# Output bias on GpSimd, later sample state, later stage transposes and a split last norm in an eight-core decoder layer

## The chip, the cores and the metric

The kernel runs on all eight cores of one Trainium2 chip. The prompt batch of eight sequences is split, one sequence of 2048 tokens per core, with 16 decode ("sample") tokens beside it. The metric is the device time of the slowest core in microseconds (us). Some executions fall into a slower state in which the cores of one die, or of both, run at a lower granted clock. A time given for a run is the median of its fast executions.

The engines in the profile: PE is TensorE's matmul, PEld its weight load, DVE is VectorE, ACT is ScalarE, POOL is GpSimd, SP is SyncE. L457 means line 457 of that kernel's file. The change shifts line numbers, so the same work has two names:

| work | before | changed |
|---|---|---|
| up/gate matmuls (SwiGLU) | L457 | L482 |
| silu of the gate (ACT) | L462 | L487 |
| down matmuls | L521 | L546 |
| combined input projection | L576 | L604 |
| width-31 conv as matmuls | L694 | L722 |
| output projection | L806 | L834 |
| bias matmuls / bias add | L809 | L846 |
| rstd (one over the standard deviation) of the conv norm (POOL) | L768, L770 | L796, L798 |
| transposes of normalised or loaded tiles | L396 | L395 |

## The reference, cut to what matters

```python
x = layer_norm(ALPHA * x + 0.5 * swiglu(x, f1_wg, f1_wu, f1_wd), ln_f1_g, ln_f1_b)
# token_mixers: z = x @ w_in + b_in, split into five parts
#   u = a_val * sigmoid(a_gate);  ua = silu(layer_norm(conv31(u) + b_dw_a))
#   v = g_c * b_val;              ub = g_b * conv3(v)
m = concatenate([ua, ub]) @ w_o + b_o
x = layer_norm(ALPHA * x + m, ln_mix_g, ln_mix_b)
x = layer_norm(ALPHA * x + 0.5 * swiglu(x, f2_wg, f2_wu, f2_wd), ln_f2_g, ln_f2_b)
# sample tokens: the same, the convolutions continue from state_conv_a and state_conv_b
```

d_model is 1024, the SwiGLU width 2816, one layer.

## The kernel before

A core's tokens are worked in two blocks. The stages follow one another on PE: start and first up stage, first down stage, first mixer stage, second down stage, second mixer stage, third down stage, last up and down stages, last norm. A mixer stage weaves the mixer of one block (conv part "C", output-projection part "E") into the up matmuls of another. The weave is made by `merge`: each side step carries a number, the share of up groups that may follow it. An up group is the 16 gate and up matmuls of one weight chunk on one group of tokens. In the program every engine has its own list of instructions, and a DMA stands in the list of the engine that issues it: most weights in POOL's, almost everything else in SP's.

```python
        def merge(items, side):
            credit = 0.0
            items = list(items)
            for th, gap in side:
                th()
                credit += gap
                while credit >= 1.0 - 1e-9 and items:
                    items.pop(0)()
                    credit -= 1.0
            # ... the rest of the items
```

The output bias was added by two rank-2 matmuls per tile (the bias split in two bf16 rows), behind the 16 matmuls of the output projection:

```python
            def S3(t):
                # ...
                    for k in (4, 5, 6, 7, 0, 1, 2, 3):
                        for h in range(2):
                            e.matmul(ps[...], lhsT=lhs(k), rhs=wo[:, k, ...], start=(k == 4), stop=False)
                    for h in range(2):
                        ins = e.matmul(ps[...], lhsT=ones2[0:2, :n], rhs=bo2[0:2, ...], start=False, stop=True)

            def A(i):
                if 0 <= i - 1 < nt:
                    S2(tl[i - 1])          # transposes back, silu on ACT
                if i < nt:
                    S1(tl[i])              # transposes, statistics on DVE, rstd on POOL, normalise on ACT
                    xslot[i] = load_xr(tl[i], ...)     # reload the residual
```

The conv input takes a detour: DVE writes u, SP stores it to memory (`uscr`), SP loads it back four times, shifted (`R2`), and only then the conv matmuls of that channel group (`tD`) can run, some steps later. Of the steps, `tA` stores u and `tB` reloads it; there are four channel groups, called channels below. The start of a mixer stage:

```python
        side = [(lambda: None, 2.0), (lambda p=pend: xpose(*p, mb()), 1.0)] + mixer(0, 0, 0.8, 0.9, 1.5)
        merge(up_items(0, 1), side)
        # ...
        side = [(lambda: None, 1.0), (lambda p=pend: xpose(*p, mb()), 0.5)] + mixer(1, 1, 0.5, 0.6, 1.0)
        merge(up_items(1, 0), side)
```

`xpose(*pend)` transposes the last normalised tile of the down stage before. At the start, `consts()` made the two bias rows with DVE operations and small SP DMAs; behind them, SP issued the loads of the sample state.

Of the kernel before, what the change touches and what calls it, by code (L numbers as in the profile page):

```python
# [6 lines left out]
F32 = mybir.dt.float32  # L7
# [5 lines left out]
D = 1024  # L13
# [158 lines left out]
def build_nc():  # L172
# [36 lines left out]
    with stack:  # L209
# [7 lines left out]
        E4 = sb("E4", [128, 4, 32], F32)  # L217
        dgb = sb("dgb", [128, 2, 8 * 128], BF16)
        bo2 = sb("bo2", [2, D], BF16)
        ones2 = sb("ones2", [2, 128], BF16)  # L220
        lnb = sb("lnb", [128, 2, D], F32)
# [200 lines left out]
        def ln_tail(ctx):  # L422
# [6 lines left out]
                op0=ALU.mult, op1=ALU.add), reads=[("xr", s), ("rs", m), ("lnb", 1)], writes=[("xr", s)])  # L429

        def store_xr(t, s, dst, wtok=()):
            n = tok(t)[1]
            P.op("sp", lambda e: e.dma_start(out=dst, in_=xr[:n, s, :]), reads=[("xr", s)], writes=list(wtok),
                 dma="xr_st%d" % s)
# [59 lines left out]
        def down(which, b, in_scale, eps, final, npar=0, aux=None):  # L494
# [40 lines left out]
            for i, t in enumerate(tl):  # L535
                n = tok(t)[1]
                if npar:
                    if i == 0:
                        for c in range(0, 16, 2):
                            for ii in range(npar):  # L540
                                mms(ii, c, c + 2)
                    mms(i, 16 if i < npar else 0, NFC)
                elif i == 0:
                    for c in range(0, NFC, 2):
                        mms(i, c, c + 2)
                else:  # L546
                    mms(i, 0, NFC)
                pre(i + nsk)
                if pend is not None:
                    xpose(*pend, tb())  # L550
                    pend = None
                for h in aux.get(i, ()):
                    h()
                ctx = ln_head(t, slots[i], pairs[i], in_scale, eps)
                ln_tail(ctx)
                if final:
                    (tok0, n) = tok(t)
                    store_xr(t, slots[i], yp[tok0:tok0 + n, :] if t < 16 else ys[:, :])
                else:
                    c = cast_xb(t, slots[i])  # L560
                    store_xr(t, slots[i], spill(0, t), [("x1", t)])
                    pend = (t, c)
            return pend

        def unit_C(u):
# [112 lines left out]
            def tD0(ch):  # L678
                ds_ = ch % 2
                wcol = C_WP + ch * 32  # L680
                P.op("dve", lambda e: e.tensor_tensor(
                    out=dgb[:, ds_, :].rearrange("p (q g c) -> p q g c", q=8, g=4),
                    in0=E4[:, :, :].unsqueeze(1).to_broadcast([128, 8, 4, 32]),
                    in1=cst[:, wcol:wcol + 32].rearrange("p (q g) -> p q g", q=8).unsqueeze(3).to_broadcast([128, 8, 4, 32]),
                    op=ALU.mult), reads=["E4", "cst"], writes=[("dgb", ds_)])

            def tD(ch):
                bk = mb()
                ds_ = ch % 2

# [22 lines left out]
            for ch in range(4):  # L713
                prev = ch - 1
                out.append(th(lambda ch=ch: tD0(ch), lambda ch=ch: tA(ch)))
                if prev >= 0:
                    out.append(th(lambda p=prev: tD(p)))
                out.append(th(lambda ch=ch: tB(ch), lambda ch=ch: rep_in(ch), lambda ch=ch: tB2(ch)))
                out.append(th(lambda ch=ch: tG(ch)))
# [17 lines left out]
        def unit_E(u):  # L737
# [57 lines left out]
            def S3(t):  # L795
# [7 lines left out]
                def pe(e):  # L803
                    for k in (4, 5, 6, 7, 0, 1, 2, 3):
                        for h in range(2):
                            e.matmul(ps[:n, (4 + h) * 512:(5 + h) * 512], lhsT=lhs(k), rhs=wo[:, k, h * 512:(h + 1) * 512],  # L806
                                     start=(k == 4), stop=False)
                    for h in range(2):
                        ins = e.matmul(ps[:n, (4 + h) * 512:(5 + h) * 512], lhsT=ones2[0:2, :n],  # L809
                                       rhs=bo2[0:2, h * 512:(h + 1) * 512], start=False, stop=True)  # L810
                    return ins
                rt = [("catS", k) for k in range(8)] if t == 16 else \
                    [("catA", k, t % 4) for k in range(4)] + [("catB", par, k) for k in range(4)]
                P.op("pe", pe, reads=rt + ["wo", "ones2", "bo2"] + ME, writes=pst(4, 2))

            def A(i):
                if 0 <= i - 1 < nt:
                    S2(tl[i - 1])
                if i < nt:
                    S1(tl[i])  # L820
# [126 lines left out]
        P.op("dve", lambda e: e.tensor_copy(out=ident_bf[:], in_=ident[:]), reads=["ident"], writes=["ident_bf"])  # L947
        P.op("dve", lambda e: e.memset(ones2[:], 1.0), writes=["ones2"])
        P.op("dve", lambda e: e.memset(haloU[:], 0.0), writes=[("haloU", c) for c in range(4)])
# [5 lines left out]
        def consts():  # L955
# [3 lines left out]
                                                  op0=ALU.mult), reads=["cst"], writes=["hbg"])  # L959
            s1, s2 = xrr(), xrr()  # L960
            hl = xb[0:1, 0, :]
            c = xbr()
            c2_ = xbr()
            P.op("sp", lambda e: e.dma_start(out=xr[0:1, s1, :], in_=bod), writes=[("xr", s1)], dma="c_bo")
            P.op("dve", lambda e: e.tensor_copy(out=xb[0:1, c, :], in_=xr[0:1, s1, :]), reads=[("xr", s1)], writes=[("xb", c)])
            P.op("dve", lambda e: e.tensor_copy(out=xr[0:1, s2, :], in_=xb[0:1, c, :]), reads=[("xb", c)], writes=[("xr", s2)])
            P.op("dve", lambda e: e.tensor_tensor(out=xb[0:1, c2_, :], in0=xr[0:1, s1, :], in1=xr[0:1, s2, :], op=ALU.subtract),
                 reads=[("xr", s1), ("xr", s2)], writes=[("xb", c2_)])
            P.op("sp", lambda e: e.dma_start(out=bo2[0:1, :], in_=xb[0:1, c, :]), reads=[("xb", c)], writes=[("bo2", 0)],
                 dma="c_bo2a")  # L970
            P.op("sp", lambda e: e.dma_start(out=bo2[1:2, :], in_=xb[0:1, c2_, :]), reads=[("xb", c2_), ("bo2", 0)],
                 writes=["bo2"], dma="c_bo2b")

# [18 lines left out]
        ss = sample_state()  # L992
        side = [(lambda: (consts(), ss[0](), load_ln(0)), 2)]
        for i in range(11):
            side.append((lambda i=i: load_wd(0, i), 1.0))
            side.append((ss[1 + i] if i < len(ss) - 1 else (lambda: None), 2.2))
        merge(up_items(0, 0)[4:], side)
# [20 lines left out]
        while wstate["f"] < NWIN:  # L1018
            fetch_win()
        side = [(lambda: None, 2.0), (lambda p=pend: xpose(*p, mb()), 1.0)] + mixer(0, 0, 0.8, 0.9, 1.5)  # L1020
        merge(up_items(0, 1), side)
        load_ln(0)
        pend = down(0, 1, 2.0 * ALPHA, 4.0 * EPS, False, npar=3)
        side = [(lambda: None, 1.0), (lambda p=pend: xpose(*p, mb()), 0.5)] + mixer(1, 1, 0.5, 0.6, 1.0)
        merge(up_items(1, 0), side)
# [77 lines left out]
```

## Time and profile before

| | before |
|---|---|
| time | 1313.61 and 1314.78 us; a third run, 1399.56, was slow |
| spans of the cores in the profiled run | 1295.9 to 1312.2 us |
| PE busy | 95% |

Three lines of the page of the kernel before: the span, the busy times (us, share, instructions), and the shares of the chain of waits that ended last.

```profile
span 1312.2 us, 20168 instructions; the slowest of 8 cores (1295.9 to 1312.2 us)
PE 1240.5 (95%) x7262; PEld 645.5 (49%) x7262; DVE 527.4 (40%) x856; ACT 273.9 (21%) x460; POOL 211.3 (16%) x361
PE 87%; DMA 6%; DVE 2%; issue 2%; ACT 1%; POOL 1%; SPq 0%; POOLq 0%; DVEq 0%; ACTq 0%
```

PE is the bound. What can be won is PE work and PE waits. The view of waits, PE alone, kernel before (who waited for what: us in total, times, longest):

```profile
PE ps L893 <- DMA sb_hT<-sca: 12.9, 1, 12.9
PE ps L396 <- ACT sb_xb L384: 11.4, 5, 5.1
PE ps L396 <- DMA sb_hT<-xp: 9.3, 2, 8.3
PE ps L694 <- DMA sb_RW<-uscr: 6.7, 2, 5.1
PE ps L457 <- ACT sb_sg L462: 2.2, 3, 1.4
```

The first is the sample state, the fourth the conv input, the last the silu. The timeline around the start, kernel before (start in us, duration, engine, line, operation, output<-input, count; in brackets the idle time before it and what ended it):

```profile
39.98 0.64 SPq L969 DMA_DIRECT2D sb_bo<-sb_xb  x1
46.28 0.52 SPq L971 DMA_DIRECT2D sb_bo<-sb_xb  x1
46.85 3.33 SPq L880 DMA_DIRECT2D sb_hT<-sca  x4
61.90 1.03 PE L893 MATMUL ps<-sb_ident,sb_hT 128*128 128x128 f32 x4 [12.90 <-DMA sb_hT<-sca]
```

SP issued the sample load (46.85) only behind the two bias rows (39.98 and 46.28), which waited for DVE. PE timeline of one output projection, kernel before:

```profile
377.44 3.62 PE L806 MATMUL ps<-sb_wo,sb_RW 128*128 128x512 bf16 x16
380.99 0.60 PE L809 MATMUL ps<-sb_bo,sb_ones 2*128 2x512 bf16 x2
381.52 2.56 PE L457 MATMUL ps<-sb_xT,sb_ring 128*128 128x352 bf16 x16
```

Matmuls overlap in the record, so the cost of a group is read from start to start: the two bias matmuls take 381.52 - 380.99 = 0.53 us.

### The profile page before, as it was taken

To read this page: it belongs to the slowest core of one execution; us is meant where nothing else is said; L and a number is where in the kernel's file an instruction comes from. 1 tells how busy PE (TensorE), PEld (TensorE's weight loads), DVE (VectorE), ACT (ScalarE), POOL (GpSimd) and SP (SyncE) were. 2 spreads that over 40 slices of the span, in tenths; PEclk is the share of its full clock that TensorE was granted. 3 is DMA by queue.
4 is the path that set the end of the run, shared out by engine and by line. 5 is a ranking of instruction groups with operands and counts; after the bars stand their busy time and mean duration, and the time that the engine had idled before them with its cause. 6 is when DMAs were issued, how large, how long until landed. Compare 5 with 4: busy or idle time off the path is not lost.

```text
span 1312.2 us, 20168 instructions; the slowest of 8 cores (1295.9 to 1312.2 us)
## 1 busy us (share of the span) xinstructions
PE 1240.5 (95%) x7262; PEld 645.5 (49%) x7262; DVE 527.4 (40%) x856; ACT 273.9 (21%) x460; POOL 211.3 (16%) x361
## 2 busy tenths in 40 slices
PE   5599999999999999998989899999999999999996
PEld 4244444445555556553444344445444456666443
DVE  0222124544445544515544345543633632222454
ACT  2111112231123313301121123313420011111000
POOL 2011102211122112111111112102220110000011
PEclk9899999999999999999999999999999999999999
DMA  9686769448865686793237856546777344442122
GB/s 137 132 180 112 123 111 179 135 118 148 168 124 126 136 164 118 159 198 107 67 102 142 163 110 134 123 89 132 148 177 146 128 113 80 69 79 33 51 82 81
DMA packets 65172, 161.54 MB, mean 123 GB/s; under 512 B 6882, under 2 KB 17506, under 8 KB 65059
## 3 DMA queue, kind: packets, MB, share of 16 engines
q0 software_dynamic: 36832, 90.75, 42.8%
q1 hardware_dynamic: 28243, 69.51, 16.6%
q8 instruction: 60, 0.98, 0.3%
q14 instruction: 37, 0.30, 0.1%
HBM read 223.24 MB, written 28.70 MB: 192 GB/s over the span
## 4 chain that ended last, share of the span: by engine, by line
PE 87%; DMA 6%; DVE 2%; issue 2%; ACT 1%; POOL 1%; SPq 0%; POOLq 0%; DVEq 0%; ACTq 0%
PE ps L457 44%; PE ps L521 23%; PE ps L576 10%; PE ps L806 4%; PE ps L694 2%; DMA sb_RW<-wd 2%; PE ps L396 2%; DMA sb_RW<-uscr 1%; DMA sb_hT<-sca 1%; DMA uscr<-sb_RW 1%; DMA sb_ring<-wgu 1%; PE ps L809 1%; PE ps L783 1%; PE ps L758 1%; DVE sb_xr L427 1%
## 5 line engine op out<-in xcount | busy, mean ns | idle before, releaser
L457 PE MATMUL ps<-sb_xT,sb_ring 128*128 128x352 bf16 (+3 forms) x3568 | 639.3, 338 | 13.9 <-ACT sb_xT L400 7.0
L457 PEld LDWEIGHTS ps<-sb_xT,sb_ring 128*128 128x128 bf16 x3568 | 347.9, 99 | 284.8 <-issue 30.6
L521 PE MATMUL ps<-sb_RW,sb_hT 128*128 128x512 bf16 (+1 forms) x1496 | 327.4, 380 | 0.6 <-DMA sb_RW<-wd 0.6
L464 DVE TENSOR_TENSOR sb_hT<-sb_sg,ps 128x352 bf16<-128x352 f32 (+3 forms) x223 | 129.0, 579 | 456.9 <-PE ps L457 399.1
L521 PEld LDWEIGHTS ps<-sb_RW,sb_hT 128*128 128x128 bf16 (+1 forms) x1496 | 145.2, 98 | 175.7 <-issue 3.5
L462 ACT ACTIVATE sb_sg<-ps 128x352 f32<-128x352 f32 (+3 forms) x223 | 113.5, 510 | 497.0 <-PE ps L457 395.9
L576 PE MATMUL ps<-sb_xT,sb_wring 128*128 128x512 bf16 (+1 forms) x800 | 150.4, 340 | 2.0 <-DVE sb_hT L464 1.3
L408 DVE SCALAR_TENSOR_TENSOR sb_xr<-sb_xr,ps 128x1024 f32<-128x1024 f32 (+1 forms) x51 | 62.2, 1219 | 172.4 <-PE ps L521 154.1
L337 POOL DMA_DIRECT2D sb_ring<-wgu x90 | 49.9, 558 | 412.4 <-PE ps L457 373.9
L576 PEld LDWEIGHTS ps<-sb_xT,sb_wring 128*128 128x128 bf16 x800 | 68.5, 98 | 78.6 <-issue 5.5
L416 POOL TENSOR_SCALAR sb_mv<-sb_mv 128x1 f32<-128x1 f32 (+1 forms) x51 | 16.0, 314 | 383.5 <-DVE sb_mv L414 383.4
L427 DVE SCALAR_TENSOR_TENSOR sb_xr<-sb_xr,sb_mv,sb_lnb 128x1024 f32<-128x1024 f32 (+1 forms) x51 | 65.5, 1284 | 21.4 <-POOL sb_mv L418 18.4
L350 POOL DMA_DIRECT2D sb_wring<-win x80 | 43.4, 543 | 174.1 <-PE ps L576 152.0
L384 ACT ACTIVATE sb_xb<-sb_xr 128x1024 bf16<-128x1024 f32 (+1 forms) x34 | 36.0, 1058 | 164.2 <-DVE sb_xr L427 164.2
L412 DVE BATCH_NORM_STATS2 sb_stt<-sb_xr 128x6 f32<-128x512 f32 (+1 forms) x102 | 65.6, 684 | 5.3
L424 DVE SCALAR_TENSOR_TENSOR sb_xr<-sb_xr,sb_mv,sb_lnb 128x1024 f32<-128x1024 f32 (+1 forms) x51 | 66.0, 1294 | 4.1
L400 ACT ACTIVATE sb_xT<-ps 128x1024 bf16<-128x1024 bf16 (+1 forms) x51 | 48.7, 978 | 72.0 <-PE ps L396 71.8
L806 PE MATMUL ps<-sb_wo,sb_RW 128*128 128x512 bf16 x256 | 57.9, 379 | 0.0
L418 POOL TENSOR_TENSOR sb_mv<-sb_mv,sb_neghalf 128x1 f32<-128x1 f32 (+1 forms) x51 | 53.8, 1055 | 7.9 <-POOL sb_mv L416 0.9
L806 PEld LDWEIGHTS ps<-sb_wo,sb_RW 128*128 128x128 bf16 x256 | 24.9, 98 | 29.0 <-issue 0.4
L694 PE MATMUL ps<-sb_RW,sb_dgb 128*32 128x512 bf16 x512 | 31.8, 392 | 7.5 <-DMA sb_RW<-uscr 6.7
L396 PE MATMUL ps<-sb_ident_bf,sb_xb 128*128 128x128 bf16 (+1 forms) x272 | 20.7, 219 | 11.4 <-ACT sb_xb L384 11.4
(82 smaller groups left out, 394.5 us busy)
## 6 DMA issues: line engine op xcount, KB each, us to landing
sb_ring<-wgu POOLq DMA_DIRECT2D x86, 512.0 KB, 5.8
sb_wring<-win POOLq DMA_DIRECT2D x80, 256.0 KB, 5.5
sb_RW<-wd POOLq DMA_DIRECT2D x33, 512.0 KB, 8.2
sb_RW<-uscr SPq DMA_DIRECT2D x64, 135.0 KB, 4.5
sb_xr<-xp SPq DMA_DIRECT2D x16, 512.0 KB, 7.1
x1s<-sb_xr SPq DMA_DIRECT2D x16, 512.0 KB, 3.0
sb_xr<-x1s SPq DMA_DIRECT2D x16, 512.0 KB, 6.5
x2s<-sb_xr SPq DMA_DIRECT2D x16, 512.0 KB, 3.1
```

The costliest lines, as they stand in the source:

```text
L408: P.op("dve", lambda e: e.scalar_tensor_tensor(out=xr[:n, s, :], in0=xr[:n, s, :], scalar=in_scale, in1=ps[:n, bk * 512:(bk + 2) * 512], o ...
L412: P.op("dve", lambda e, h=h: e.bn_stats(out=stt[:n, m, h, :], in_=xr[:n, s, h * 512:(h + 1) * 512]), reads=[("xr", s)], writes=[("stt", m, ...
L418: P.op("pool", lambda e: e.tensor_tensor(out=mv[:n, m, 2:3], in0=mv[:n, m, 3:4], in1=neghalf[:n, 0:1], op=ALU.pow), reads=[("ve", m), "neg ...
L424: P.op("dve", lambda e: e.scalar_tensor_tensor(out=xr[:n, s, :], in0=xr[:n, s, :], scalar=mv[:n, m, 0:1], in1=lnb[:n, 0, :], op0=ALU.subtr ...
L427: P.op("dve", lambda e: e.scalar_tensor_tensor(out=xr[:n, s, :], in0=xr[:n, s, :], scalar=mv[:n, m, 2:3], in1=lnb[:n, 1, :], op0=ALU.mult, ...
L457: ins = e.matmul(bank(bk, n), lhsT=ring[:, s, c:c + 128], rhs=xT[:, k, tok0:tok0 + n], start=(k == 0), stop=(k == KC - 1))
L462: P.op("act", lambda e: e.activation(out=sg[:, q, :n], in_=bank(bg, n), func=AF.Silu), reads=pst(bg), writes=[("sg", q)])
L464: P.op("dve", lambda e: e.tensor_tensor(out=hT[:, f, l0:l0 + n], in0=sg[:, q, :n], in1=bank(bu, n), op=ALU.mult), reads=[("sg", q)] + pst( ...
L521: ins = e.matmul(ps[:n, (yb + h) * 512:(yb + h + 1) * 512], lhsT=hT[:, f, l0:l0 + n], rhs=wd[:, f, h * 512:(h + 1) * 512], start=(f == 0), ...
L576: ins = e.matmul(bank(bk, n), lhsT=wring[:, slot, k * 128:(k + 1) * 128], rhs=xT[:, k, tok0:tok0 + n], start=(k == 0), stop=(k == KC - 1))
L694: ins = e.matmul(ps[32 * g_:32 * g_ + 32, bk * 512:(bk + 1) * 512], lhsT=dgb[:, ds_, q * 128 + 32 * g_: q * 128 + 32 * g_ + 32], rhs=R2[:, ...
L806: e.matmul(ps[:n, (4 + h) * 512:(5 + h) * 512], lhsT=lhs(k), rhs=wo[:, k, h * 512:(h + 1) * 512], start=(k == 4), stop=False)
```

## The change

Its intent: take the bias off PE; let the sample loads be issued at once and use their data later; let PE do other work while the last tile of a stage is still being normalised; and start the last norm on the half that is finished first. To make room for the bias row in all partitions, the conv weights (`dgb`) lose their second buffer, and are built a step later.

```diff
-                            e.matmul(..., start=(k == 4), stop=False)
-                    for h in range(2):
-                        ins = e.matmul(..., lhsT=ones2[0:2, :n], rhs=bo2[0:2, ...], start=False, stop=True)
+                            ins = e.matmul(..., start=(k == 4), stop=(k == 3))
...
             def A(i):
                 if 0 <= i - 1 < nt:
                     S2(tl[i - 1])
+                if 0 <= i - 1 < nt:
+                    n, s = tok(tl[i - 1])[1], xslot[i - 1]
+                    P.op("pool", lambda e: e.tensor_tensor(out=xr[:n, s, :], in0=xr[:n, s, :], in1=boa[:n, :], op=ALU.add), ...)
                 if i < nt:
                     S1(tl[i])
                     xslot[i] = load_xr(tl[i], spill(0, tl[i]), [("x1", tl[i])])
...
-        # consts(): bias split in two bf16 rows by DVE, two small SP DMAs
+            P.op("sp", lambda e: e.dma_start(out=boa[:, :], in_=bod.to_broadcast([128, D])), ...)
+            P.op("dve", lambda e: e.tensor_scalar(out=boa[:, :], in0=boa[:, :], scalar1=1.0 / ALPHA, ...), ...)
...
-        side = [(lambda: (consts(), ss[0](), load_ln(0)), 2)]
-        for i in range(11):
-            side.append((lambda i=i: load_wd(0, i), 1.0))
-            side.append((ss[1 + i] if i < len(ss) - 1 else (lambda: None), 2.2))
+        ev = [(0, lambda: (consts(), ss[0](), load_ln(0)))]
+        ev += [(5 + 2 * k, ss[k]) for k in range(1, 6)] + [(3.5 + 3.3 * i, lambda i=i: load_wd(0, i)) for i in range(11)]
+        # sorted; the share between two events is the difference of their numbers
...
-        side = [(lambda: None, 2.0), (lambda p=pend: xpose(*p, mb()), 1.0)] + mixer(0, 0, 0.8, 0.9, 1.5)
+        side = [(lambda: None, 2.0)] + mixer(0, 0, 0.8, 0.9, 1.5)
+        side.insert(5, (lambda p=pend: xpose(*p, mb()), 0.2))
...
-        side = [(lambda: None, 1.0), (lambda p=pend: xpose(*p, mb()), 0.5)] + mixer(1, 1, 0.5, 0.6, 1.0)
+        side = [(lambda: None, 1.0)] + mixer(1, 1, 0.5, 0.6, 1.0)
+        side.insert(5, (lambda p=pend: xpose(*p, mb()), 0.1))
...
-        dgb = sb("dgb", [128, 2, 8 * 128], BF16)
+        dgb = sb("dgb", [128, 1, 8 * 128], BF16)
...
+        # last tile: down matmuls of one output half after the other; ln_halves() works, scales
+        # and stores each half by itself, with the statistics joined in between
```

More of the change, by code (lines that the diff above doesn't have):

```diff
@@ L217, in build_nc @@
         E4 = sb("E4", [128, 4, 32], F32)
-        dgb = sb("dgb", [128, 2, 8 * 128], BF16)
-        bo2 = sb("bo2", [2, D], BF16)
-        ones2 = sb("ones2", [2, 128], BF16)
+        dgb = sb("dgb", [128, 1, 8 * 128], BF16)
+        boa = sb("boa", [128, D], F32)
         lnb = sb("lnb", [128, 2, D], F32)
@@ L429, in ln_tail, with ln_halves @@
                 op0=ALU.mult, op1=ALU.add), reads=[("xr", s), ("rs", m), ("lnb", 1)], writes=[("xr", s)])
+        def ln_halves(s, bk, in_scale, eps, dst):
+            m = mvr()
+            hs = lambda h: slice(h * 512, (h + 1) * 512)
+            for h in range(2):
+                P.op("dve", lambda e, h=h: e.scalar_tensor_tensor(
+                    out=xr[:, s, hs(h)], in0=xr[:, s, hs(h)], scalar=in_scale, in1=bank(bk + h),
+                    op0=ALU.mult, op1=ALU.add), reads=[("xr", s)] + pst(bk + h), writes=[("xrh", h)])
+                P.op("dve", lambda e, h=h: e.bn_stats(out=stt[:, m, h, :], in_=xr[:, s, hs(h)]),
+                     reads=[("xrh", h)], writes=[("stt", m, h)])
+            P.op("dve", lambda e: e.bn_aggr(out=mv[:, m, 0:2], in_=stt[:, m, :, :].rearrange("p a b -> p (a b)")),
+                 reads=[("stt", m, 0), ("stt", m, 1)], writes=[("mv", m)])
+            P.op("dve", lambda e: e.tensor_scalar(out=mv[:, m, 3:4], in0=mv[:, m, 1:2], scalar1=eps, scalar2=None,
+                                                  op0=ALU.add), reads=[("mv", m)], writes=[("ve", m)])
+            P.op("pool", lambda e: e.tensor_tensor(out=mv[:, m, 2:3], in0=mv[:, m, 3:4], in1=neghalf[:, 0:1], op=ALU.pow),
+                 reads=[("ve", m), "neghalf"], writes=[("rs", m)])
+            for h in range(2):
+                P.op("dve", lambda e, h=h: e.scalar_tensor_tensor(
+                    out=xr[:, s, hs(h)], in0=xr[:, s, hs(h)], scalar=mv[:, m, 0:1], in1=lnb[:, 0, hs(h)],
+                    op0=ALU.subtract, op1=ALU.mult), reads=[("xrh", h), ("mv", m), ("lnb", 0)], writes=[("xrh", h)])
+            for h in range(2):
+                P.op("dve", lambda e, h=h: e.scalar_tensor_tensor(
+                    out=xr[:, s, hs(h)], in0=xr[:, s, hs(h)], scalar=mv[:, m, 2:3], in1=lnb[:, 1, hs(h)],
+                    op0=ALU.mult, op1=ALU.add), reads=[("xrh", h), ("rs", m), ("lnb", 1)], writes=[("xrh", h)])
+                P.op("sp", lambda e, h=h: e.dma_start(out=dst[:, hs(h)], in_=xr[:, s, hs(h)]), reads=[("xrh", h)],
+                     dma="last%d" % h)
         def store_xr(t, s, dst, wtok=()):
@@ L546, in down @@
                 else:
-                    mms(i, 0, NFC)
+                    mms(i, 0, NFC, h_outer=(final and b == 1 and i == len(tl) - 1))
                 pre(i + nsk)
@@ L553, in down @@
                     h()
+                if final and b == 1 and i == len(tl) - 1:
+                    ln_halves(slots[i], pairs[i], in_scale, eps, yp[t * 128:(t + 1) * 128, :])
+                    continue
                 ctx = ln_head(t, slots[i], pairs[i], in_scale, eps)
@@ L678, in tD0 @@
             def tD0(ch):
-                ds_ = ch % 2
+                ds_ = 0
                 wcol = C_WP + ch * 32
@@ L688, in tD @@
                 bk = mb()
-                ds_ = ch % 2
+                ds_ = 0
                 def pe(e):
@@ L714, in unit_C @@
                 prev = ch - 1
-                out.append(th(lambda ch=ch: tD0(ch), lambda ch=ch: tA(ch)))
+                out.append(th(*([lambda: tD0(0)] if ch == 0 else []), lambda ch=ch: tA(ch)))
                 if prev >= 0:
                     out.append(th(lambda p=prev: tD(p)))
-                out.append(th(lambda ch=ch: tB(ch), lambda ch=ch: rep_in(ch), lambda ch=ch: tB2(ch)))
+                out.append(th(*([lambda ch=ch: tD0(ch)] if ch else []), lambda ch=ch: tB(ch), lambda ch=ch: rep_in(ch), lambda ch=ch: tB2(ch)))
                 out.append(th(lambda ch=ch: tG(ch)))
@@ L805, in pe @@
                         for h in range(2):
-                            e.matmul(ps[:n, (4 + h) * 512:(5 + h) * 512], lhsT=lhs(k), rhs=wo[:, k, h * 512:(h + 1) * 512],
-                                     start=(k == 4), stop=False)
-                    for h in range(2):
-                        ins = e.matmul(ps[:n, (4 + h) * 512:(5 + h) * 512], lhsT=ones2[0:2, :n],
-                                       rhs=bo2[0:2, h * 512:(h + 1) * 512], start=False, stop=True)
+                            ins = e.matmul(ps[:n, (4 + h) * 512:(5 + h) * 512], lhsT=lhs(k),
+                                           rhs=wo[:, k, h * 512:(h + 1) * 512], start=(k == 4), stop=(k == 3))
                     return ins
@@ L813, in S3 @@
                     [("catA", k, t % 4) for k in range(4)] + [("catB", par, k) for k in range(4)]
-                P.op("pe", pe, reads=rt + ["wo", "ones2", "bo2"] + ME, writes=pst(4, 2))
+                P.op("pe", pe, reads=rt + ["wo"] + ME, writes=pst(4, 2))
             def A(i):
@@ L818, in A @@
                     S2(tl[i - 1])
+                if 0 <= i - 1 < nt:
+                    n, s = tok(tl[i - 1])[1], xslot[i - 1]
+                    P.op("pool", lambda e: e.tensor_tensor(out=xr[:n, s, :], in0=xr[:n, s, :], in1=boa[:n, :], op=ALU.add),
+                         reads=[("xr", s), "boa"], writes=[("xr", s)])
                 if i < nt:
@@ L947, in build_nc @@
         P.op("dve", lambda e: e.tensor_copy(out=ident_bf[:], in_=ident[:]), reads=["ident"], writes=["ident_bf"])
-        P.op("dve", lambda e: e.memset(ones2[:], 1.0), writes=["ones2"])
         P.op("dve", lambda e: e.memset(haloU[:], 0.0), writes=[("haloU", c) for c in range(4)])
@@ L959, in consts @@
                                                   op0=ALU.mult), reads=["cst"], writes=["hbg"])
-            s1, s2 = xrr(), xrr()
-            hl = xb[0:1, 0, :]
-            c = xbr()
-            c2_ = xbr()
-            P.op("sp", lambda e: e.dma_start(out=xr[0:1, s1, :], in_=bod), writes=[("xr", s1)], dma="c_bo")
-            P.op("dve", lambda e: e.tensor_copy(out=xb[0:1, c, :], in_=xr[0:1, s1, :]), reads=[("xr", s1)], writes=[("xb", c)])
-            P.op("dve", lambda e: e.tensor_copy(out=xr[0:1, s2, :], in_=xb[0:1, c, :]), reads=[("xb", c)], writes=[("xr", s2)])
-            P.op("dve", lambda e: e.tensor_tensor(out=xb[0:1, c2_, :], in0=xr[0:1, s1, :], in1=xr[0:1, s2, :], op=ALU.subtract),
-                 reads=[("xr", s1), ("xr", s2)], writes=[("xb", c2_)])
-            P.op("sp", lambda e: e.dma_start(out=bo2[0:1, :], in_=xb[0:1, c, :]), reads=[("xb", c)], writes=[("bo2", 0)],
-                 dma="c_bo2a")
-            P.op("sp", lambda e: e.dma_start(out=bo2[1:2, :], in_=xb[0:1, c2_, :]), reads=[("xb", c2_), ("bo2", 0)],
-                 writes=["bo2"], dma="c_bo2b")
+            P.op("sp", lambda e: e.dma_start(out=boa[:, :], in_=bod.to_broadcast([128, D])), writes=["boa"], dma="c_bo")
+            P.op("dve", lambda e: e.tensor_scalar(out=boa[:, :], in0=boa[:, :], scalar1=1.0 / ALPHA, scalar2=None,
+                                                  op0=ALU.mult), reads=["boa"], writes=["boa"])
         def x0pose(t):
@@ L992, in build_nc @@
         ss = sample_state()
-        side = [(lambda: (consts(), ss[0](), load_ln(0)), 2)]
-        for i in range(11):
-            side.append((lambda i=i: load_wd(0, i), 1.0))
-            side.append((ss[1 + i] if i < len(ss) - 1 else (lambda: None), 2.2))
+        ev = [(0, lambda: (consts(), ss[0](), load_ln(0)))]
+        ev += [(5 + 2 * k, ss[k]) for k in range(1, 6)] + [(3.5 + 3.3 * i, lambda i=i: load_wd(0, i)) for i in range(11)]
+        ev.sort(key=lambda v: v[0])
+        side = [(th, (ev[k + 1][0] if k + 1 < len(ev) else t0) - t0) for k, (t0, th) in enumerate(ev)]
         merge(up_items(0, 0)[4:], side)
```

## The prediction

> **What bounds it.** TensorE. The page gives PE 95% busy (1240.5 of 1312.2 us); the chain of waits is 87% PE. Only less PE work or fewer PE waits can pay. The table of PE waits on the slowest core: sample-state load 12.9 us (one wait; 9.7 to 13.2 over the cores), the cast of a normalised tile 11.4, x loads at the start 9.3.
>
> **Steps.**
>
> 1. *Bias matmuls.* 34 rank-2 matmuls. The PE timeline shows the pair adding 0.53 us behind each group of 16 output-projection matmuls (380.99 to 381.52), so 17 x 0.53 = 9.0 us of PE work. In line on PE: -9 us.
>
> 2. *Bias on GpSimd.* 17 adds of 128x1024 f32. The Trainium skill, "GPSIMD Engine Reference", section 3.1, gives 4.5 us for a 2048-wide two-input add; I estimate 2.3 us each, on an engine busy 16%. They sit before the small rstd instructions and weight-fetch issues and need the reloaded residual, which SP sometimes issues late. Mostly hidden: +2 us.
>
> 3. *Start.* Before, SyncE waited 37 us for the bias split on DVE, then 6.2 us for its DMA; the sample-state load was issued only at 46.9 and landed at 61.7, while PE waited from 49.0. Slow matmuls after it (48 in 13.3 us, not 10.4) cost 3 us more. The change removes the block and moves the first sample transposes from 3 to 7 items later, so the wait goes: -16 us. But the sample load (0.94 MB) and the new 0.5 MB bias broadcast are now issued in the first 7 us, where the DMA engines are full (share 0.75 to 1.07 by the windows) with x and the first weights. The skill, "DMA: Bandwidth & Descriptors", section "Queues, rings and completion order", says an engine alternates between queues by packet; 1.45 MB at the 165 GB/s of that window is an estimated 9 us of DMA time. The state's second load must still wait for an x transpose (shared rows), so what is queued behind it does not collide. I expect the first matmul group to start 4 to 5 us later (13.9 to about 18) and the preamble to end 6 to 7 us later: +7. Net -9 us (-4 to -14).
>
> 4. *Stage transposes.* After the second down stage PE waits 2.4 us for the last tile's cast, then runs 16 matmuls in 5.2 us, not 3.5: -4 us. After the first down stage the moved transpose did not wait: 0.
>
> 5. *Last norm.* The tail from the last matmul to the end is 10.2 us. Halving hides half the residual and statistics (1.25 us) and shortens the last store: -2 us.
>
> 6. *Single conv-weight buffer*: 0.
>
> Sum: -9 + 2 - 9 - 4 - 2 = -22 us: **1292 us**, 8 in 10 within **1283 to 1302**. Chances: faster by over 2% 0.25, within 2% 0.73, slower by over 2% 0.02.
>
> **What would show it.** Step 1: the bias group gone, PE busy down about 9 us. Step 2: the adds near 2.3 us, PE waits on GpSimd-fed ScalarE output up under 3 us. Step 3: no sample-state wait; start waits on x and the first weights up 4 to 8 us. Step 4: no cast wait before the mixer of block 1. Step 5: last matmul to end near 8 us.
>
> **What would make it wrong.** A start that suffers less from the shared DMA engines (then 1286 or below), or a slow row broadcast; GpSimd adds that stall PE in the mixer.

## More of the kernel before

Timeline of one rstd of the conv norm in the first mixer stage, kernel before. DVE finishes the variance, POOL follows at once, ACT normalises (L773) and then does the silu (L462):

```profile
511.01 0.15 DVE L766 TENSOR_SCALAR sb_mvc<-sb_mvc 128x1 f32<-128x1 f32 x1
511.38 0.56 POOL L768 TENSOR_TENSOR sb_mvc<-sb_mvc,sb_neghalf 128x1 f32<-128x1 f32 x1 [2.40 <-DVE sb_mvc L766]
512.48 0.78 ACT L773 ACTIVATE sb_RW<-ps,sb_mvc 128x512 f32<-128x512 f32 x1 [1.48 <-POOL sb_mvc L770]
513.15 0.44 ACT L462 ACTIVATE sb_sg<-ps 128x336 f32<-128x336 f32 x1
```

Timeline of the first conv group of that stage, kernel before: a weight fetch by POOL, the store of u, its reload, and the conv matmuls, which do not wait:

```profile
290.30 0.62 POOL L337 DMA_DIRECT2D sb_ring<-wgu  x1 [7.72 <-PE ps L457]
294.21 0.33 SPq L650 DMA_DIRECT2D uscr<-sb_RW  x1
302.11 2.00 SPq L659 DMA_DIRECT2D sb_RW<-uscr  x4
310.33 1.91 PE L694 MATMUL ps<-sb_RW,sb_dgb 128*32 128x512 bf16 x32
```

## The result, and the profile after

The changed kernel takes 1308.12 us (median of 4, 1306.82 to 1311.23); the kernel before, in the same rounds, 1313.61 (median of 3 fast runs, 1312.88 to 1314.78). The ratio is 0.9961, with a 95% interval of 0.9937 to 0.9984. Ratios here are the mean time of one kernel's fast runs over that of the other's of the same rounds, so they are not quite the ratio of the medians quoted. The change is faster, but by 5 to 6 us and not by the 22 forecast.

The page of the changed kernel (the profiled core lost 102 matmul records, seen in x7126 against x7228 weight loads, so its PE figure is a little low):

```profile
span 1305.3 us, 20027 instructions; the slowest of 8 cores (1293.1 to 1305.3 us)
PE 1229.8 (94%) x7126; PEld 645.7 (49%) x7228; DVE 535.7 (41%) x857; ACT 271.4 (21%) x460; POOL 260.2 (20%) x377
PE 83%; DMA 6%; DVE 3%; issue 3%; POOL 2%; ACT 1%; SPq 0%; DVEq 0%; POOLq 0%; ACTq 0%
```

The chain is less PE (83% against 87%) though the kernel is faster: waits have come in. The view of waits, PE alone, changed kernel:

```profile
PE ps L395 <- DMA sb_hT<-xp: 11.4, 4, 8.0
PE ps L722 <- DMA sb_RW<-uscr: 9.9, 3, 3.7
PE ps L482 <- ACT sb_sg L487: 9.0, 7, 2.2
PE ps L395 <- ACT sb_xb L383: 8.8, 4, 5.4
```

The sample-state wait is gone, the bias group is gone, and two waits have grown: the conv input from 6.7 to 9.9, the silu from 2.2 to 9.0. To find the stage in which time came and went, the traces of all eight cores were cut at the first and last weight load of each stage. Means over the cores of one profiled execution each, in us; the short gaps between the stages are left out, and the third column splits the prediction by stage (half of the adds' +2 in each mixer stage, 8 of the 17 bias pairs in the first and 9 in the second):

| stage | before | changed | predicted change | measured change |
|---|---|---|---|---|
| start and first up stage, to its last weight load | 192.4 | 183.3 | -9 | -9.1 |
| first down stage | 81.6 | 82.0 | 0 | +0.4 |
| first mixer stage | 290.8 | 296.2 | -3 | **+5.4** |
| second down stage | 96.6 | 97.3 | 0 | +0.7 |
| second mixer stage | 305.0 | 305.6 | -8 | **+0.6** |
| third down stage | 76.6 | 75.8 | 0 | -0.8 |
| last up and down stages | 243.8 | 244.3 | 0 | +0.5 |
| from the last weight load to the end | 10.8 | 9.3 | -2 | -1.5 |

The start gave what was forecast. The mixer stages gave nothing, and lost 17 us against the forecast. Timeline of one output-projection tile in the first mixer stage, changed kernel, to be laid beside the rstd lines of before:

```profile
518.35 0.15 DVE L794 TENSOR_SCALAR sb_mvc<-sb_mvc 128x1 f32<-128x1 f32 x1
518.64 2.35 POOL L846 TENSOR_TENSOR sb_xr<-sb_xr,sb_boa 128x1024 f32<-128x1024 f32 x1
520.95 0.56 POOL L796 TENSOR_TENSOR sb_mvc<-sb_mvc,sb_neghalf 128x1 f32<-128x1 f32 x1
522.04 0.78 ACT L801 ACTIVATE sb_RW<-ps,sb_mvc 128x512 f32<-128x512 f32 x1 [3.72 <-POOL sb_mvc L798]
522.71 0.46 ACT L487 ACTIVATE sb_sg<-ps 128x352 f32<-128x352 f32 x1
529.06 1.90 PE L482 MATMUL ps<-sb_xT,sb_ring 128*128 128x352 bf16 x8 [2.15 <-ACT sb_sg L487]
```

The variance was ready at 518.50, but POOL was in the bias add until 521; the rstd started 2.6 us after the variance was started on DVE, instead of 0.4. Not every tile is hit: over all cores this distance is above 1.5 us in 56 of 136 tiles (at most 3.2), and in none of the kernel before. ACT idles 3.72 us for it (1.48 before), its silu comes late, DVE's product and norm come late behind the silu, and in the end PE waits 2.15 us for a later silu. Timeline of the first conv group, changed kernel:

```profile
282.97 0.33 SPq L678 DMA_DIRECT2D uscr<-sb_RW  x1
288.25 0.53 POOL L336 DMA_DIRECT2D sb_ring<-wgu  x1 [1.75 <-PE ps L482]
288.75 3.33 SPq L687 DMA_DIRECT2D sb_RW<-uscr  x4
301.15 3.52 PE L722 MATMUL ps<-sb_RW,sb_dgb 128*32 128x512 bf16 x32 [3.05 <-DMA sb_RW<-uscr]
```

Here PE waits 3.05 us, and the 32 conv matmuls behind the wait take 3.52 us instead of 1.91: they run at half speed (granted clock 0.50 from 301.15 to 303.70; 1.00 from 310.33 to 312.24 in the kernel before). The 512 KB weight fetch is now issued 0.5 us before the reload; in the kernel before it was 11.8 us before it. (256 KB fetches of the input projection, left out here, stand around both.)

At the start, changed kernel, the sharing of the DMA engines that was forecast is seen: the bias row and the sample state are issued at 2.5 to 5.9 us, and PE waits for the third x tile, which it had not before:

```profile
2.45 0.43 SPq L988 DMA_DIRECT2D sb_boa<-bo  x1
2.93 2.96 SPq L909 DMA_DIRECT2D sb_hT<-sca  x4
15.10 3.85 PE L482 MATMUL ps<-sb_xT,sb_ring 128*128 128x256 bf16 x16 [3.40 <-DMA sb_ring<-wgu]
19.73 1.01 PE L395 MATMUL ps<-sb_ident_bf,sb_hT 128*128 128x128 bf16 x8 [0.78 <-DMA sb_hT<-xp]
```

### The profile page after: what moved, and what is told of

It reads as the page before. It is cut to its first block, busy times and chain, and to the rows that moved or that the text cites. A ratio compares the mean times of both kernels' runs of the same rounds, so it can differ in the third digit from the quotient of the medians.

```text
span 1305.3 us, 20027 instructions; the slowest of 8 cores (1293.1 to 1305.3 us)
## 1 busy us (share of the span) xinstructions
PE 1229.8 (94%) x7126; PEld 645.7 (49%) x7228; DVE 535.7 (41%) x857; ACT 271.4 (21%) x460; POOL 260.2 (20%) x377
## 4 chain that ended last, share of the span: by engine, by line
PE 83%; DMA 6%; DVE 3%; issue 3%; POOL 2%; ACT 1%; SPq 0%; DVEq 0%; POOLq 0%; ACTq 0%
PE ps L482 42%; PE ps L546 24%; PE ps L604 8%; PE ps L834 4%; PE ps L722 3%; DMA sb_RW<-uscr 2%; PE ps L395 1%; DMA uscr<-sb_RW 1%; DMA sb_hT<-xp 1%; DMA sb_wring<-xp 1%; ACT sb_xT L399 1%; DMA sb_wring<-win 1%; DVE sb_xr L426 1%; DVE sb_stt L411 0%; DVE sb_xr L407 0%
## 5 line engine op out<-in xcount | busy, mean ns | idle before, releaser
L482 PE MATMUL ps<-sb_xT,sb_ring 128*128 128x512 bf16 (+3 forms) x3530 | 636.9, 338 | 24.5 <-ACT sb_sg L487 9.0
L604 PE MATMUL ps<-sb_xT,sb_wring 128*128 128x512 bf16 (+1 forms) x777 | 147.0, 337 | 4.2 <-ACT sb_RW L801 1.6
L415 POOL TENSOR_SCALAR sb_mv<-sb_mv 128x1 f32<-128x1 f32 (+1 forms) x50 | 46.6, 932 | 366.2 <-DVE sb_mv L413 366.1
L426 DVE SCALAR_TENSOR_TENSOR sb_xr<-sb_xr,sb_mv,sb_lnb 128x1024 f32<-128x1024 f32 (+1 forms) x50 | 64.2, 1284 | 32.3 <-POOL sb_mv L417 29.4
L722 PE MATMUL ps<-sb_RW,sb_dgb 128*32 128x512 bf16 x512 | 35.4, 425 | 9.9 <-DMA sb_RW<-uscr 9.9
L846 POOL TENSOR_TENSOR sb_xr<-sb_xr,sb_boa 128x1024 f32<-128x1024 f32 (+1 forms) x17 | 40.1, 2360 | 0.2
L417 POOL TENSOR_TENSOR sb_mv<-sb_mv,sb_neghalf 128x1 f32<-128x1 f32 (+1 forms) x50 | 30.2, 604 | 7.4
```

Of the source, the lines that this page charges most:

```text
L426: P.op("dve", lambda e: e.scalar_tensor_tensor(out=xr[:n, s, :], in0=xr[:n, s, :], scalar=mv[:n, m, 2:3], in1=lnb[:n, 1, :], op0=ALU.mult, ...
L482: ins = e.matmul(bank(bk, n), lhsT=ring[:, s, c:c + 128], rhs=xT[:, k, tok0:tok0 + n], start=(k == 0), stop=(k == KC - 1))
L604: ins = e.matmul(bank(bk, n), lhsT=wring[:, slot, k * 128:(k + 1) * 128], rhs=xT[:, k, tok0:tok0 + n], start=(k == 0), stop=(k == KC - 1))
L722: ins = e.matmul(ps[32 * g_:32 * g_ + 32, bk * 512:(bk + 1) * 512], lhsT=dgb[:, ds_, q * 128 + 32 * g_: q * 128 + 32 * g_ + 32], rhs=R2[:, ...
```

## The experiments

Theories for the loss in the mixer stages:

- A: the GpSimd add stands ahead of the rstd in POOL's order, so ScalarE and then PE wait.
- B: moving the stage transposes changed the shares in the weave, so conv steps have less PE work between the store of their input and its use.
- C: the single conv-weight buffer holds up DVE.
- D (later): the load of the norm rows at the start of the mixer stage slows the reload.

All runs passed the comparison of results; so did e2, which is wrong on purpose. So the comparison does not see this bias, and in the other runs it does not prove the bias right. Stage times below are means over the eight cores of one profiled execution. e1 to e4, e5 to e8 and e9 to e11 ran on three different chips; only the ratios are against the kernel before in the same rounds. The scatter of the stages can be read from runs that do not touch them: the first mixer stage is 290.8, 290.1 and 290.5 us in the kernel before, e4 and e7, but the second is 305.0, 306.4 and 308.0; and e1 and e10, which have the same second mixer stage, read 300.5 and 304.5. In the second mixer stage a difference under about 4 us is therefore not settled by one trace.

### e1: the add behind the rstd (A)

```diff
                     S2(tl[i - 1])
-                if 0 <= i - 1 < nt:
-                    P.op("pool", ... bias add of tile i - 1 ...)
                 if i < nt:
                     S1(tl[i])
+                if 0 <= i - 1 < nt:
+                    P.op("pool", ... bias add of tile i - 1 ...)
+                if i < nt:
                     xslot[i] = load_xr(...)
```

> The changed kernel with one line moved: the GpSimd bias add of a tile is put behind the two small rstd instructions of the next tile instead of ahead of them. Theory A (the 2.36 us add delays the rstd, so ScalarE, whose silu PE waits for): the waits of up matmuls for ScalarE's silu in the two mixer stages fall from 9.0 us (7 waits) to under 4, mixer stages 5 to 9 us shorter together, time near 1300. Theory B (the moved stage transposes shifted the interleave, and the conv input comes too late): nothing changes but the silu waits, time within 2 us of 1308. Theory C (single conv-weight buffer holds up DVE): the same as B.

1298.28 us, ratio 0.987 (0.9836 to 0.9903). The mixer stages are 3.9 and 5.1 us shorter than in the changed kernel, 9.0 together (all PE waits in them, mean of the cores, fell by 3.8 and 2.9). Timeline of one tile in this run (core 4): the rstd starts 0.37 us after the variance, and the add behind it:

```profile
514.73 0.15 DVE L794 TENSOR_SCALAR sb_mvc<-sb_mvc 128x1 f32<-128x1 f32 x1
515.10 0.56 POOL L796 TENSOR_TENSOR sb_mvc<-sb_mvc,sb_neghalf 128x1 f32<-128x1 f32 x1 [0.21 <-DVE sb_mvc L794]
516.07 2.34 POOL L848 TENSOR_TENSOR sb_xr<-sb_xr,sb_boa 128x1024 f32<-128x1024 f32 x1
```

The silu wait of PE on the slowest core is 2.4 us (3 waits). The rstd now starts at most 0.7 us after the variance in all 136 tiles. Theory A holds, for about 9 us of the loss.

### e2: no add at all (A; wrong on purpose)

```diff
-                if 0 <= i - 1 < nt:
-                    P.op("pool", ... bias add of tile i - 1 ...)
```

> The changed kernel without the GpSimd bias adds (wrong result on purpose: the output bias is missing). It gives the whole cost of the adds. Theory A: 6 to 11 us less than the changed kernel, 1297 to 1302, and at most 2 us below the run with the late add. Theories B and C: under 3 us less.

1297.43 us, ratio 0.9853 (0.9825 to 0.9882); mixer stages 4.8 and 5.7 us shorter than in the changed kernel, 10.5 together. The adds cost 10.5 us where they stood and about 1.5 us where e1 puts them. What hurt was the place and not the work: 17 adds are 40 us of POOL time in the changed kernel and in e1.

### e3: the old shares of up work behind the stage transposes (B)

```diff
-        side.insert(5, (lambda p=pend: xpose(*p, mb()), 0.2))
+        side.insert(5, (lambda p=pend: xpose(*p, mb()), 1.0))
...
-        side.insert(5, (lambda p=pend: xpose(*p, mb()), 0.1))
+        side.insert(5, (lambda p=pend: xpose(*p, mb()), 0.5))
```

> The changed kernel with the stage transposes still late, but with their old share of up work behind them (1.0 and 0.5 up groups instead of 0.2 and 0.1), so that conv steps and up groups interleave as before. Theory B: in the first mixer stage the waits of conv matmuls for their replicated input (2 waits, 6 to 8 us, each followed by matmuls at half speed) shrink to under 2 us, that stage 6 to 10 us shorter; the second about unchanged (-2 to +2); time near 1300. Theories A and C: within 2 us of 1308.

1299.07 us (three fast runs; a fourth was slow), ratio 0.9879 (0.9839 to 0.992). The first mixer stage falls from 296.2 to 288.2, its conv-input waits from 5.4 us to 0.1 (mean of the cores). The second falls by 1.3 only, and the third down stage is 2.8 us longer: PE waits there for its weights. Theory B holds in the first mixer stage, for 8 us; in the second it gains nothing.

How the shares do it is in `merge`, which can be counted by hand. Between storing the fourth channel's input (`tA`) and using it (`tD`) lay four up groups in the kernel before; with 2.0 + 0.2 in place of 2.0 + 1.0, the phase moves by 0.2 and three are left; in e3 there are four again. In the first channel there are three before, three in the changed kernel and four in e3, but there the reload itself became slower. In us from the last weight load of the down stage (core 5 before, core 4 of the others):

| first mixer stage | reload issued | landed | conv starts | PE wait |
|---|---|---|---|---|
| before, first channel | 25.0 | 32.3 | 33.2 | 0 |
| changed, first channel | 20.5 | 32.7 | 32.9 | 3.05 |
| e3, first channel | 19.9 | 31.3 | 32.1 | 0 |
| before, fourth channel | 72.9 | 81.6 | 82.7 | 0 |
| changed, fourth channel | 77.0 | 87.4 | 87.6 | 3.09 |
| e3, fourth channel | 71.5 | 78.2 | 81.5 | 0 |

Issuing the reload 4.5 us sooner did not make it land sooner. In the changed kernel it runs beside a 512 KB weight fetch. e3 has that neighbour too (its fetch is issued within 0.2 us of the reload) and lands at 31.3; it does not wait because one more up group covers it. Timeline of e3, core 4:

```profile
283.79 1.76 SPq L687 DMA_DIRECT2D sb_RW<-uscr  x4
283.90 0.54 POOL L336 DMA_DIRECT2D sb_ring<-wgu  x1 [1.74 <-PE ps L482]
295.97 1.91 PE L722 MATMUL ps<-sb_RW,sb_dgb 128*32 128x512 bf16 x32
```

The DMA view of the stretch from issue to landing shows what shared the engines with this reload: 0.37 MB of weights in the kernel before (DMA engines busy 0.71 of the time), 1.50 MB in the changed kernel (1.01), 1.26 MB in e3 (0.91).

### e4: the single conv-weight buffer alone, on the kernel before (C)

```diff
-        dgb = sb("dgb", [128, 2, 8 * 128], BF16)
+        dgb = sb("dgb", [128, 1, 8 * 128], BF16)
...  (built in the step of tB instead of tA, as in the change)
```

> The kernel before with only the conv-weight buffer made single and its build moved to the later step. Theory C: mixer stages 3 to 10 us longer, time 1318 to 1325. Theories A and B: within 2 us of the kernel before, mixer stages as before (290.8 and 305.0 us, mean of the cores).

1314.63 us, ratio 0.9995 (0.9954 to 1.0036); mixer stages 290.1 and 306.4 against 290.8 and 305.0. Theory C falls.

### e5: both repairs

e1 and e3 together.

> The changed kernel with both repairs, the late bias add and the old share of up work behind the stage transposes. If A and B are separate costs they add up: first mixer stage about 284 us (mean of the cores; 296.2 in the changed kernel, 292.3 and 288.2 with one repair each), second about 299.5, time 1290 to 1294. If they are the same slack counted twice, 1297 to 1300.

1296.81 us (three fast runs; a fourth was slow), ratio 0.9862 (0.9846 to 0.9879). Mixer stages 285.1 and 301.1. In the first the two repairs nearly add up (11.1 us against 3.9 + 8.0); in the second it is 4.5 against 5.1 + 1.3, within the scatter. The total misses the expected 1290 to 1294: the third down stage is 80.1 instead of 75.8 us (PE waits 3.0 us there for its weights, mean of the cores; none in the changed kernel), and the start of this run was 1.3 us slower. By the expectation as written this time would speak for one slack counted twice; the stage times show that it is two costs and a new wait.

### e6: the moved transposes alone, on the kernel before (B)

```diff
-        side = [(lambda: None, 2.0), (lambda p=pend: xpose(*p, mb()), 1.0)] + mixer(0, 0, 0.8, 0.9, 1.5)
+        side = [(lambda: None, 2.0)] + mixer(0, 0, 0.8, 0.9, 1.5)
+        side.insert(5, (lambda p=pend: xpose(*p, mb()), 0.2))
...  (the second stage change likewise)
```

> The kernel before with only the stage-change transposes moved back, as the change moves them. Theory B: the conv input waits appear in the first mixer stage without anything else of the change, which becomes 5 to 9 us longer (290.8 to about 297), the second 0 to 4 us shorter; time 1315 to 1322. If the shift needed the other parts (more DMA traffic, less PE work) to hurt, both stages stay or shorten and the time is 1309 to 1314.

1318.14 us (three fast runs; two were slow), ratio 1.0032 (1.0012 to 1.0052): slower, with nothing else changed. The first mixer stage is 6.1 us longer, with 6.2 us of conv-input waits that the kernel before does not have. The second is 1.2 us longer, within its scatter, and not shorter: the wait for the cast fell from 3.2 to 0.8 us, that for the conv input rose from 3.8 to 7.0. The view of waits, PE alone, of this run:

```profile
PE ps L694 <- DMA sb_RW<-uscr: 13.9, 4, 4.9
```

### e7: the later sample steps alone, on the kernel before

The diff is the `ev` hunk of the change.

> The kernel before with only the sample-state steps moved later; the bias split that blocks SyncE stays. The load still lands near 62 us and the first sample transposes now come after 7 up groups, at about 62: the 12.9 us wait should shrink to under 2, the start should not lose anything to shared DMA (first up group still near 12.5 us), so the first up stage ends 11 to 15 us earlier than before (192.4), more than the 9 of the changed kernel; time 1300 to 1304. If the unblocked queue was what mattered, the wait stays above 8 us.

1305.72 us (three fast runs, 1303.56 to 1310.31; a fourth was slow), ratio 0.9938 (0.9911 to 0.9965). The first up stage ends at 180.9 instead of 192.4, 11.5 us sooner, and 2.4 us sooner than with the whole change. The sample wait is 2.5 us on the slowest core, a little over the expected 2 (none on four cores, 5.3 on one). So this part alone is worth at least as much as the whole change. Of its 11.5 us, 3.0 are given back in the second mixer stage and 1.2 in the third down stage, and the time just misses the expected 1300 to 1304. Nothing in this edit touches the second mixer stage, whose length varies from core to core (301 to 309 us in the kernel before) and between runs; the 3.0 may be scatter.

### e8: both repairs, and the sample load and bias row behind the x tiles

```diff
             def loads():
+                P.op("sp", ... load of scb into sbst ...)      # must wait for an x transpose: shared rows
                 for r in range(4):
                     P.op("sp", ... loads of sca ...)
-                P.op("sp", ... load of scb into sbst ...)
...
-        ev = [(0, lambda: (consts(), ss[0](), load_ln(0)))]
+        ev = [(0, lambda: (consts(), ss[0](), load_ln(0), load_boa())), (26, scale_boa)]
```

> Both repairs, and the sample load and the bias row are issued only behind the load that waits for an x transpose, so they do not share the DMA engines with x and the first weights. If that sharing cost 5 to 7 us at the start (preamble end 42.8 to 44 us instead of 37.7), the preamble ends near 38 us again, with no sample wait, and the time is 4 to 6 us below the run with both repairs, 1285 to 1289. If not, no difference.

1290.18 us, ratio 0.9817 (0.9803 to 0.9832), 6.6 us below e5. The preamble (to the third weight chunk, mean of the cores) ends at 37.5 us instead of 44.7 in e5. Timeline of this run: the sample load is issued at 26.6, behind the load that waits for x:

```profile
12.91 3.57 PE L482 MATMUL ps<-sb_xT,sb_ring 128*128 128x256 bf16 x16 [1.27 <-ACT sb_xT L399]
26.22 0.34 SPq L908 DMA_DIRECT2D sb_hT<-scb  x1
26.60 2.40 SPq L911 DMA_DIRECT2D sb_hT<-sca  x4
32.44 1.03 SPq L991 DMA_DIRECT2D sb_boa<-bo  x1
```

The sharing at the start cost 7.2 us in e5. The prediction had estimated 7 for it; in the changed kernel the preamble ended 5.1 us later than before (42.8 against 37.7).

### e9: norm rows loaded later, on the changed kernel (D)

```diff
-        side = [(lambda: (mode("RMC"), mode("RME"), load_ln(1)), 0.0)]
+        side = [(lambda: (mode("RMC"), mode("RME")), 0.0)]
...  (load_ln(1) with the first step of unit_E)
```

> The changed kernel with one load moved: the 1 MB of norm rows for the mixer is issued at the first output-projection tile instead of at the start of the mixer stage, where it runs beside the conv staging stores and reloads. Theory D (that load holds up the staging DMA): from the moved transpose to the first conv matmul the staging takes 4 to 6 us less, the waits for the replicated input (5.4 us in the first mixer stage, 5.9 in the second, mean of the cores) fall below 3 each, time 1299 to 1304. If the weight fetches or something else hold it up: waits within 1 us of those of the changed kernel, time 1306 to 1310.

1311.6 us, ratio 0.9956 (0.9922 to 0.9991). In the first mixer stage nothing changes (conv-input waits 6.3 against 5.4 us); the trace of the changed kernel shows why: the rows have landed 13.8 us into the stage, the reload is issued at 20.5. In the second mixer stage the waits fall from 5.9 to 2.8 us and the stage by 4.7. The total is no better. Theory D falls for the first mixer stage. For the second it stays open: the wait at the first channel falls here from 5.6 to 2.1 us, but the same edit made between e10 and e11 takes it only from 6.0 to 5.2, and the stage varies from 297.6 to 307.3 over the cores of this run.

### e10 and e11: towards a better kernel

e10 is e8 with the second share back at 0.1; e11 is e10 with the norm rows late.

> The run with both repairs and the later sample load, with the share of up work behind the second stage transpose put back to 0.1 (there the old share gained nothing and the second down stage behind it started without its weights). If that is the cause of the longer down stage: 78.1 falls to about 75.8, the mixer stage before it stays at 300 to 301, time 1287 to 1289. If not: 78 again and 1290.

1286.58 us, ratio 0.9773 (0.9744 to 0.9802), just below the expected 1287 to 1289. But the reason is not shown: the third down stage is 77.1 (not 75.8), and the second mixer stage is 304.5, above the expected 300 to 301, with 8.5 us of conv-input waits. By the traces the two stages together are 2.5 us longer than in e8, which ran on another chip; the profiled execution was also the slowest of the four (1289.91 us).

> The same with the norm rows moved as well. By theory D the second mixer stage loses the rest of its conv input waits (about 5 us and the slow matmuls behind them): 1280 to 1285. Otherwise as the run without it, 1287 to 1290.

1284.58 us, ratio 0.9755 (0.9728 to 0.9782), the fastest kernel, though its interval overlaps that of e10. The time is inside the expected 1280 to 1285. The second mixer stage is 299.9 and the third down stage 76.0; 6.1 us of conv-input waits are left in the second mixer stage, so the gain is smaller than theory D had it.

## Why the prediction was wrong, point by point

- **Step 1, bias matmuls, -9 us.** Right in kind, and hidden in the result; no run takes the pairs out alone. With both repairs (e5) the first mixer stage is 5.6 us below the kernel before at the same PE waits (7.3 against 7.4 us); its 8 pairs were to give 4.2.
- **Step 2, bias on GpSimd, +2 us. This failed.** The add itself was sized well: 2.36 us measured against 2.3. "Mostly hidden" was wrong, although the prediction had named the rstd behind it. Where the add stands, it delays the rstd (by over 1 us in 56 of 136 tiles), and ScalarE passes that on to the silu and PE. Measured: 9.0 us (e1) to 10.5 (e2). A place after the rstd would have made "+2" true.
- **Step 3, start, -9 us.** Right: -9.1, with some luck in the number. The preamble ended 5.1 us later (forecast 6 to 7), so the rest of the stage gained 14.2 and not the 16 forecast; the two misses cancel. By e8 the sharing of the DMA engines cost 7.2 us. What the prediction did not see is that the later sample steps would have been enough without the early load (e7: -11.5).
- **Step 4, stage transposes, -4 and 0 us. This failed.** In the first mixer stage the move costs 8.0 us (e3) or 6.1 (e6), not 0: the prediction asked whether the moved transpose waited, and not what the share it carried did to the steps behind it. In the second the cast wait did go (3.2 to 1.0 us), but PE then waited for the conv input (3.8 to 5.9 us; 1.5 to 5.6 at the first channel, 2.4 to 0.3 at the fourth): a wait moved, not removed. It is not lost cover here: counted through `merge`, no channel of the second stage has fewer up groups between store and use than before.
- **Step 5, last norm, -2 us.** Right: -1.5.
- **Step 6, single conv-weight buffer, 0.** Right (e4).

So -22 was forecast. The adds cost 7 to 8.5 us more than said, the transposes 8 more in the first mixer stage and 4 more in the second; the start and the end came as said. That is 19 to 20 us, somewhat more than the 16 to 17 that are missing; the rest is within the spread of the mixer stages. What stays open is what makes the first reload of a mixer stage land late. The trace shows the weight fetches beside it. The Trainium skill, "DMA: Bandwidth & Descriptors", section "Queues, rings and completion order", says that a DMA engine takes the queues in turn, packet by packet; no run here shows the turns, and none took those fetches away.

The half-speed matmuls behind a wait are part of the conv-input losses above. The Trainium skill, "TensorE: Matmul & The Clock Gate", section "What's actually happening", gives at least one idle window of about 3.4 us for the clock to halve. Over the thirteen profiled kernels and all cores, the 32 conv matmuls (slow: over 1.8 us instead of 1.32, first to last weight load) were slow behind 6 of 185 waits of 0.5 to 2.5 us, 21 of 41 of 2.5 to 3.4 us, 31 of 40 of 3.4 to 4.5 us, and 58 of 58 above that. So the size agrees, but half of the waits just under the page's figure had slow matmuls behind them. The wait of 3.05 us shown above cost 4.7 us: 3.05, and 3.52 instead of 1.91 for the matmuls.

## What to carry to other kernels

An instruction moved to an idle engine is not hidden because that engine is idle on average: ask what stands behind it in that engine's order, and put it after the short instruction that others wait for. In a hand-woven schedule, a step that is moved takes its share of cover with it; check the distance between each load and its use again after every move. When a wait is removed, look at which wait ends next before counting it, and keep early loads out of the stretch in which the DMA engines are already full.

## What the Trainium skill lacked or had wrong

- "GPSIMD Engine Reference", section 3.1, gives 4497 ns for a two-input add of 2048 f32; half of that, as an estimate, is 2.25 us, and the 1024-wide add took 2.36 us here. It agrees. What section 4.1 lacks is that the price of an elementwise operation on GpSimd can lie in its place: the same 17 adds cost 10.5 us ahead of the rstd and about 1.5 us behind it.
- The same page has no duration for tiny instructions. Here a 128x1 tensor_scalar took 0.22 us and a 128x1 power 0.57, but one of the pair took 0.75 to 1.1 us more in the down stages: the power (1.33) in the kernel before, the tensor_scalar (1.31) in the changed one (in e3 and e8 both are off, 0.66 and 1.17) and also in e7, which changed nothing on that engine but the order of DMA issues. The pair was 0.33 us longer so, and the second down stage 0.7 us longer on every core. Why it moves is open.
- "DMA: Bandwidth & Descriptors", section "Queues, rings and completion order", says that queues are served in turn by packet, but not what that costs a transfer: the 540 KB reload landed 7.3 us after its issue beside 0.37 MB of weights and 12.2 us after it beside 1.50 MB. For the start, 1.45 MB at the 165 GB/s of that window had been estimated at 9 us; 7.2 were measured (e8 against e5).
- "TensorE: Matmul & The Clock Gate", section "What's actually happening": the idle window of about 3.4 us fits in size, but as a least value it is too long for these counts: 21 of 41 waits of 2.5 to 3.4 us were followed by matmuls at half speed. (Only the last idle stretch before the matmuls is counted, and the ends of matmuls are modelled in the trace.)
